# The transpose of a second norm vector goes to the side work of a hybrid decoder step, and its opening is reordered

## The chip, the core and the metric

The kernel runs on one core of a Trainium2 chip. Such a core has five engines, each with a queue of its own that it works off in order: TensorE (PE in the profile, with its weight loads as PEld), VectorE (DVE), ScalarE (ACT), GpSimd (POOL) and SyncE (SP). DMA transfers run beside them and are issued here by SP and ACT. The metric is the device time of one execution in microseconds (us); lower is better.

## The reference

One layer of a decoder trunk, for 1024 prompt positions and 8 x 8 sample positions, with a model width of 1024. Cut to what is computed:

```python
h = rmsnorm(x, g_norm)
bg_a, cg_a, v_a, z_a, a_b, g_b, z_b, q_x, z_x = split(h @ w_in)     # 1024 -> 3200 columns
out_a = bg_a * dwconv3(cg_a * v_a) * silu(z_a)
out_b = silu(layernorm(dwconv31(a_b * sigmoid(g_b)), ln_g, ln_b)) * silu(z_b)
m = rmsnorm(mem, g_mem)                                             # 256 memory tokens
out_x = softmax(q_x @ (m @ w_mk).T / 8) @ (m @ w_mv) * silu(z_x)    # 4 heads of 64
y = rmsnorm(x + concat(out_a, out_b, out_x) @ w_out, g_final)
```

The sample positions use cached keys, values and convolution states; the last states and the memory's keys and values are outputs too. Two norm vectors matter below: `g_norm`, which scales `x` ahead of the large projection, and `g_mem`, which scales the memory tokens.

## The kernel before

Everything lies transposed: 128 channels on the partitions, positions along a row. Each large product is made of three passes over a high and a low part of both operands (`hh`, `hl` for the activations, `wh`, `wl` for the weights): high times high, high times low weights, low activations times high weights. A part is split off by a rounding copy on ACT (or POOL) and a subtraction on DVE.

The 3200 columns of `w_in` are 25 blocks of 128 (`order`). For each block `n`, `proj` runs the three passes over eight row blocks `k` and the block is evacuated from PSUM by `evac`. The 1088 positions come in three chunks; the first five blocks (`NHEAD`) use the chunks of `HEAD`, 256, 384 and 448 positions. While `proj` runs, `side()` pops one entry of the list `steps` after every fourth product (two per pass): rescaling, splits of coming weights, parameter transposes, later the memory tokens (`mem_T`, which reads `gT[:, 8:16]`, from block 5 on), attention and the layer norm. The 31 taps of the long convolution are queued on DVE in the same way.

`startup` is the opening. It runs under `manual_schedule`: every engine does its instructions in the order in which they are written. It computes the first two chunks of the first four blocks and of block 4, and fills the third chunk's operands. Its course:

1. Loads. `graw` is an 8 x 128 tile that holds `g_norm` first and `g_mem` later. The first four blocks' weights come as eight row blocks of 128 x 512 (`hw_load`, tiles `hrw`), the first two rows of `x` as halves (`x_half`). SP issues all of them but the first `graw`, which ACT issues.
2. Five products on the identity, then the transpose of `graw` (L1012) and its copy to `gT[:, 0:8]`, then the transposes of `x` (`x0_tr`, four of eight `k` first) into PSUM banks.
3. Rows 0 and 1 of `x` aren't normalised ahead of the product. Their transposes times `g_norm` are split (`hi`, `lo`) and multiplied, group by group (`p(k, j)`: row block `k`, pass `j`, four products), while the squares are summed. The factors are brought in afterwards: `fb` holds them along rows, two transposes of `fb` give `rrow`, and the evacuations multiply by it.
4. In the same PSUM tile as those two transposes (`rps`) stands the transpose of `graw` with `g_mem`, and ACT copies `rrow` and `gT[:, 8:16]` out of it.
5. Row block 7's weights are split (`hw_hi(7)`, `hw_lo(7)`) behind that, its products end the first chunk, and the rows 2 to 4 of `x` are squared (`n1.square`), their factors computed (`n1.chain`, `n1.factor`) and applied (`n1.scale`). Block 4's weights are split (`w_hi`, `w_lo`), the four accumulators evacuated, block 4's three passes run, and the second chunk begins.

The profile's lines: L60 is every DVE operation (a wrapper), L96 every product (`mm`), L103 every transpose by `tr`, L276 the split copy of the row blocks, L188 a square on ACT, L238 `hi`, L176 and L210 loads of `x`, L270 and L293 loads of `w_in`.

## Time and profile before

| | us |
|---|---|
| median of 3 runs | 481.94 (481.22 to 482.19) |
| the profiled execution | 482.8 |
| its span, first to last instruction | 481.0 |
| busy: PE, DVE, ACT, POOL | 464.2, 324.4, 225.8, 7.1 |
| HBM read and written | 34.81 and 5.42 MB |

The granted PE clock averages 0.989 of full speed over the span. By stretches of the span, from the table of the trace by windows:

| stretch (us) | what runs | PE busy | DVE busy |
|---|---|---|---|
| 0 to 18.4 | first chunk up to the transposes of `fb` | 15.49 | 9.49 |
| 18.4 to 24.2 | | 0.24 | 0.04 |
| 24.2 to 33.2 | end of the first chunk, block 4 | 8.98 | 6.12 |
| 33.2 to 100 | other chunks, blocks 5 and on | 66.69 | 42.74 |
| 100 to 214 | long convolution beside products | 112.77 | 112.94 |
| 214 to 350 | attention, gates | 135.39 | 94.68 |
| 350 to 481 | output projection | 124.58 | 58.37 |

A busy PE is not a PE at its peak, since its products are pipelined; the idle time of an engine costs only where another waits for it.

### The profile page before, as it was taken

Reading aid. Unit: us, or ns where it says so; the run is one execution under the profiler, and the core shown is the slowest. Engines: PE = TensorE matmul, PEld = TensorE weight load, DVE = VectorE, ACT = ScalarE, POOL = GpSimd, SP = SyncE. Lnnn points to the kernel's source line nnn. Section 1 sums busy time; section 2 is a strip of 40 time slices with the busy share of each in tenths; the row PEclk is TensorE's granted clock in tenths of the full one; section 3 lists DMA queues with packets and bytes.
Section 4 is the critical chain, followed back from the end, with each engine's and each line's share of the span. In section 5 each row is a group of like instructions: output and inputs, shape, how many; then the busy total and the mean of one; then the engine's idle time right before and its main releaser. Section 6 shows DMA issues by size and latency. Waiting matters only on the chain.

```text
span 481.0 us, 7290 instructions
## 1 busy us (share of the span) xinstructions
PE 464.2 (97%) x2827; PEld 432.8 (90%) x2827; DVE 324.4 (67%) x573; ACT 225.8 (47%) x586; POOL 7.1 (1%) x22
## 2 busy tenths in 40 slices
PE   7599999999999999999999999999999999999994
PEld 7499999999999999899999999999999988888884
DVE  3465931999999999998679588832653446333434
ACT  5467722540625519655584374656863424221111
POOL 3001000000000000000000000000000000000000
PEclk9979999999999999999999999999999999999998
DMA  8940051121008300101111340113311562411111
GB/s 286 355 141 2 10 166 44 55 89 33 2 22 242 112 21 0 45 5 43 44 44 46 110 128 27 44 54 94 131 45 40 160 216 95 146 45 44 44 58 75
DMA packets 36446, 40.42 MB, mean 84 GB/s; under 512 B 1743, under 2 KB 30325, under 8 KB 36405
## 3 DMA queue, kind: packets, MB, share of 16 engines
q1 hardware_dynamic: 36397, 39.96, 26.1%
q8 instruction: 22, 0.36, 0.3%
q14 instruction: 11, 0.09, 0.1%
q10 hardware_dynamic: 16, 0.00, 0.0%
HBM read 34.81 MB, written 5.42 MB: 84 GB/s over the span
## 4 chain that ended last, share of the span: by engine, by line
PE 65%; DVE 22%; ACT 5%; DMA 4%; issue 3%; SPq 0%; DVEq 0%; ACTq 0%
PE mm L96 56%; DVE accB L60 11%; PE sd L103 4%; PE sd L96 4%; DMA graw<-in_g_mem_dram 2%; DVE tA L60 2%; DVE wl L60 2%; DMA x<-in_x_prompt_dram 1%; DVE Q L60 1%; DVE red L60 1%; DVE mx L60 1%; DMA wr<-in_w_in_dram 1%; ACT sd L870 1%; ACT junk L188 1%; DVE wml L60 1%
## 5 line engine op out<-in xcount | busy, mean ns | idle before, releaser
L96 PE MATMUL mm<-hh,wh 128*128 128x384 f32 (+3 forms) x592 | 117.0, 334 | 3.1 <-ACT wh L276 1.5
L96 PE MATMUL mm<-hl,wh 128*128 128x384 f32 (+3 forms) x592 | 117.6, 333 | 0.0
L60 DVE SCALAR_TENSOR_TENSOR accB<-u,prm,accB 128x1024 f32<-128x1024 f32 x90 | 115.0, 1279 | 1.2
L96 PE MATMUL mm<-hh,wl 128*128 128x384 f32 (+3 forms) x592 | 114.9, 331 | 0.0
L96 PEld LDWEIGHTS mm<-hh,wh 128*128 128x128 f32 x592 | 98.8, 189 | 6.6 <-ACT wh L276 1.8
L96 PEld LDWEIGHTS mm<-hl,wh 128*128 128x128 f32 x592 | 99.4, 190 | 2.0 <-issue 1.3
L96 PEld LDWEIGHTS mm<-hh,wl 128*128 128x128 f32 x592 | 99.9, 190 | 1.3 <-issue 0.3
L96 PE MATMUL mm<-woh,ml 128*128 128x512 f32 (+1 forms) x136 | 51.2, 377 | 0.0
L96 PE MATMUL mm<-wol,mh 128*128 128x512 f32 (+1 forms) x136 | 51.2, 377 | 0.0
L96 PE MATMUL mm<-woh,mh 128*128 128x512 f32 (+1 forms) x136 | 51.2, 377 | 0.0
L60 DVE TENSOR_TENSOR wl<-wr,wh 128x512 fp32r<-128x512 f32 x50 | 33.3, 685 | 10.0 <-ACT wh L276 7.4
L60 DVE TENSOR_TENSOR xres<-mm,xres 128x512 f32<-128x512 f32 (+2 forms) x19 | 12.4, 662 | 38.7 <-PE mm L96 38.5
L933 ACT ACTIVATE sd<-xres 128x512 f32<-128x512 f32 (+1 forms) x16 | 9.6, 600 | 56.9 <-DVE xres L60 56.9
L96 PEld LDWEIGHTS mm<-woh,mh 128*128 128x128 f32 x136 | 25.6, 188 | 4.7
L96 PEld LDWEIGHTS mm<-wol,mh 128*128 128x128 f32 x136 | 25.6, 188 | 4.7
L96 PEld LDWEIGHTS mm<-woh,ml 128*128 128x128 f32 x136 | 25.6, 188 | 4.6
L351 ACT ACTIVATE prod<-us,prm 128x64 f32<-128x64 f32 x93 | 23.9, 340 | 0.9 <-DVE wl L60 0.8
L701 ACT ACTIVATE P<-sd,nb 128x256 f32<-128x256 f32 x32 | 14.7, 473 | 18.8 <-DVE nb L60 18.8
L299 ACT CAST wh<-wr 128x512 fp32r<-128x512 f32 x40 | 23.3, 625 | 0.1
L499 ACT ACTIVATE sz<-mm 128x384 f32<-128x384 f32 (+1 forms) x24 | 11.3, 472 | 20.3 <-PE mm L96 20.2
L238 ACT ACTIVATE hh<-sd,gT 128x256 fp32r<-128x256 f32 (+2 forms) x24 | 12.8, 563 | 12.5 <-PE sd L103 12.2
L422 ACT ACTIVATE sig<-mm 128x384 f32<-128x384 f32 (+1 forms) x6 | 2.8, 472 | 31.3 <-PE mm L96 31.3
(204 smaller groups left out, 526.7 us busy)
## 6 DMA issues: line engine op xcount, KB each, us to landing
wr<-in_w_in_dram SPq DMA_DIRECT2D x21, 512.0 KB
wor<-in_w_out_dram SPq DMA_DIRECT2D x8, 512.0 KB
xres<-in_x_prompt_dram SPq DMA_DIRECT2D x8, 512.0 KB
out_dram<-xres SPq DMA_DIRECT2D x7, 512.0 KB
x<-in_x_prompt_dram SPq DMA_DIRECT2D x6, 512.0 KB
wr<-in_w_in_dram SPq DMA_DIRECT2D x8, 256.0 KB
cache<-in_cache_mem_k_dram SPq DMA_DIRECT2D x8, 256.0 KB
cache<-in_cache_mem_v_dram SPq DMA_DIRECT2D x8, 256.0 KB
```

What stands on the lines that cost most here:

```text
L60: r = f(*a, **k)
L96: T.matmul(out, lhsT, rhs, start=start, stop=stop)
L103: T.transpose(out, in_, ident[:n, :n])
L188: S.activation(junk[:r], self.ts[i][:r], AF.Square, accum_out=self.ss[:r, i:i + 1])
L238: S.activation(hh[k][:, off:off + n], ps[:, :n], AF.Copy, scale=gT[:, k:k + 1])
L299: S.copy(dst_hi[:, a:b], src[:, a:b])
L351: S.activation(p3[:, k, :], src, AF.Copy, scale=w[:, k0 + k:k0 + k + 1])
L422: S.activation(sig[j][:, off:off + n], ps[:, :n], AF.Sigmoid)
L499: S.activation(sz[0][:, off:off + n], ps[:, :n], AF.Silu)
L701: S.activation(P_[i][:, h * 256:h * 256 + 256], bank[h // 2][:, (h % 2) * 256:(h % 2) * 256 + 256], AF.Exp, bias=nb[:, h:h + 1], scale=SCA ...
L870: S.activation(junk[:, :384], t, AF.Square, bias=lst["nmu"][:, i:i + 1], accum_out=lst["sq"][:, i:i + 1])
L933: S.activation(junk[:rows], xr[:rows, cs], AF.Square, accum_out=ss[:rows, f:f + 1])
```

## The change

Five edits, all in the opening but for the side work's one new entry.

- The load of `g_mem` into `graw` moves on SP from behind the loads of `x` to behind `load_params()`. Its transpose and the copy to `gT[:, 8:16]` leave `rps`; the new `gm_T` does both, with a PSUM tile of its own and the copy on DVE, as the last of the entries that block 0 puts into `steps`.
- `x_half` and `hw_load` take a queue. SP issues the first half of row 0, weight row blocks 0 and 2, then the second halves; ACT issues the first half of row 1, `graw` with `g_norm`, weight row block 1, and then its first activation, which loads a table.
- The transposes of `x` for `k` = 4 to 7 stand on PE ahead of the groups `p(1, 1)` and `p(1, 2)`.
- Row 3's square moves from ACT to DVE (`square_v`), block 4's high parts from ACT to POOL. On DVE the scalings now stand ahead of block 4's low parts.
- Block 4's passes run in the order high times high, low activations times high weights, high times low weights.

```diff
+        def square_v(self, i):
+            junk = B("junk", cols=D)
+            V.tensor_tensor_reduce(
+                junk, self.ts[i], self.ts[i], 1.0, 0.0, ALU.mult, ALU.add, self.ss[:, i:i + 1]
+            )
+            dv(1130)
...
-    def x_half(i, h):
+    def x_half(i, h, q):
...
+    def gm_T():
+        ps = SD()
+        T.transpose(ps[:, 0:8], graw, ident[:8, :8])
+        V.tensor_copy(gT[:, 8:16], ps[:, 0:8])
...
-    def hw_load(k):
+    def hw_load(k, q=nc.sync):
...
     def startup():
+        V.memset(epst, EPS)
+        make_identity(nc, ident)
+        x_half(0, 0, nc.sync)
+        x_half(1, 0, nc.scalar)
+        hw_load(0)
         nc.scalar.dma_start(graw, g_norm[0].rearrange("(k p) -> k p", p=128))
-        V.memset(epst, EPS)
+        hw_load(1, nc.scalar)
         S.activation(warm, epst, AF.Sqrt)
-        make_identity(nc, ident)
+        hw_load(2)
         for i in (0, 1):
-            x_half(i, 0)
-        for k in range(3):
-            hw_load(k)
-        for i in (0, 1):
-            x_half(i, 1)
+            x_half(i, 1, nc.sync)
...
-        nc.sync.dma_start(graw, g_mem[0].rearrange("(k p) -> k p", p=128))
...
         p(2, 0)
-        p(1, 1)
-        p(1, 2)
         x_load(8)
         mem_load()
         load_params()
+        nc.sync.dma_start(graw, g_mem[0].rearrange("(k p) -> k p", p=128))
         w_load(5)
...
             for k in range(4, 8):
                 x0_tr(k, i)
+        p(1, 1)
+        p(1, 2)
...
                     tr(rps[:, i * 128:i * 128 + 128], fb[:, i * 128:i * 128 + 128], 128)
-                T.transpose(rps[:, 256:264], graw, ident[:8, :8])
                 n1.square(0)
                 rrow[0] = B("rrow", cols=RAW)
                 S.copy(rrow[0], rps[:, :RAW])
-                S.copy(gT[:, 8:16], rps[:, 256:264])
...
-        n1.square(1)
+        w_hi(4, G.tensor_copy)
+        n1.square_v(1)
         n1.square(2)
         n1.chain()
         n1.factor()
-        w_hi(4, S.copy)
+        n1.scale_act(1)
+        n1.scale(0)
+        n1.scale(2)
         w_lo(4)
-        n1.scale(0)
-        n1.scale_act(1)
-        n1.scale(2)
...
-        for j in range(3):
-            pass_(4, 0, pr4, j)
+        for j, (lo_, h) in enumerate(((False, hh), (False, hl), (True, hh))):
+            for k in range(KT):
+                mm(
+                    pr4[:, :RAW], w_block(4, k, lo_), h[k][:, :RAW],
+                    j == 0 and k == 0, j == 2 and k == KT - 1, RAW / 2.4,
+                )
...
                         steps += [mk(params_T, j), None]
+                    steps.append(gm_T)
```

## The prediction

> **What bounds the kernel now.** I began with the page: TensorE (PE) is busy nearly everywhere, and the chain that ended last (the last line) runs mostly through it, so time is to be won where PE stands still or runs slowly. The chain holds one oddity, a 4 KB load of `g_mem` with 2% of the span. (The middle line is DVE's busy tenths in 40 slices of 12 us.)

> ```profile
> PE 464.2 (97%) x2827; PEld 432.8 (90%) x2827; DVE 324.4 (67%) x573; ACT 225.8 (47%) x586; POOL 7.1 (1%) x22
> ...
> DVE  3465931999999999998679588832653446333434
> ...
> PE mm L96 56%; DVE accB L60 11%; PE sd L103 4%; PE sd L96 4%; DMA graw<-in_g_mem_dram 2%; DVE tA L60 2%; DVE wl L60 2%; DMA x<-in_x_prompt_dram 1%; DVE Q L60 1%; DVE red L60 1%; DVE mx L60 1%; DMA wr<-in_w_in_dram 1%; ACT sd L870 1%; ACT junk L188 1%; DVE wml L60 1%
> ```

> Next the same chain in order of time (start, duration, what). The first row is a weight load; then an `x` load lets the `g_mem` load go, which takes 9.20 us; the opening's products come behind it.

> ```profile
> 2.11 4.90 DMA wr<-in_w_in_dram
> 7.02 6.56 DMA x<-in_x_prompt_dram
> 13.67 9.20 DMA graw<-in_g_mem_dram
> ...
> 24.18 4.64 PE mm L96 x20
> 28.82 3.38 PE sd L96 x24
> ...
> 33.19 0.97 PE mm L96 x4
> ```

> Then the timeline around that load (start, duration, engine; in brackets idle time and what ended it).

> ```profile
> 16.53 0.64 PE L96 MATMUL mm<-hh,wh 128*128 128x256 f32 x4
> ...
> 17.01 0.64 PE L96 MATMUL mm<-hh,wl 128*128 128x256 f32 x4
> ...
> 17.97 0.38 PE L103 MATMUL sd<-ident,fb 128*128 128x128 f32 x2
> ...
> 22.91 0.23 PE L1094 MATMUL sd<-ident,graw 8*128 8x8 f32 x1 [4.56 <-DMA graw<-in_g_mem_dram]
> 23.17 0.37 ACT L1097 COPY rrow<-sd 128x256 f32<-128x256 f32 x1 [6.20 <-PE sd L1094]
> 23.44 0.17 ACT L1098 COPY gT<-sd 128x8 f32<-128x8 f32 x1
> 23.50 0.63 ACT L276 CAST wh<-wr 128x512 fp32r<-128x512 f32 x1
> 24.02 1.07 ACT L188 ACTIVATE junk<-x 128x1024 f32<-128x1024 f32 x1
> 24.16 0.69 DVE L60 TENSOR_TENSOR wl<-wr,wh 128x512 fp32r<-128x512 f32 x1 [6.64 <-ACT wh L276]
> 24.18 0.93 PEld L96 LDWEIGHTS mm<-hh,wh 128*128 128x128 f32 x4 [1.14 <-ACT wh L276]
> 24.18 1.22 PE L96 MATMUL mm<-hh,wh 128*128 128x256 f32 x4 [1.05 <-ACT wh L276]
> ...
> 26.24 0.17 DVE L60 TENSOR_SCALAR v<-ss 128x3 f32<-128x3 f32 x1 [1.39 <-ACT junk L188]
> ...
> 27.49 1.29 DVE L60 TENSOR_TENSOR wl<-wr,wh 128x512 fp32r<-128x512 f32 x2
> ...
> 28.70 1.53 DVE L60 TENSOR_SCALAR x<-x,y,t 128x1024 f32<-128x1024 f32 x2
> ...
> 30.14 1.08 DVE L60 TENSOR_TENSOR u<-mm,rrow 128x256 f32<-128x256 f32 x3
> ```

> PE is in order, so the transpose of `graw` for `g_mem`, which nothing needs before the memory tokens are transposed, stops PE; `rrow`'s copy reads the same PSUM tile and waits with it, and the split of the seventh weight row block stands behind that copy on ScalarE (ACT). From the transposes' end at 18.35 to 24.18 nothing useful runs. The table of stretches (duration, busy time by engine, then granted PE clock, DMA share, GB/s) shows the second cost.

> ```profile
> 22.50:23.00 0.50, 0.09 (x1) 0.09 (x1) 0.00 (x0) 0.00 (x0) 0.00 (x0) 1.00 0.79 238
> ...
> 24.00:25.00 1.00, 0.82 (x4) 0.82 (x5) 0.69 (x1) 1.00 (x3) 0.09 (x1) 0.50 0.91 168
> ...
> 29.50:29.75 0.25, 0.25 (x3) 0.25 (x3) 0.25 (x2) 0.00 (x0) 0.00 (x0) 0.50 0.62 154
> ...
> 30.00:30.50 0.50, 0.50 (x7) 0.50 (x6) 0.50 (x3) 0.00 (x0) 0.00 (x0) 1.00 0.95 344
> ```

> After the 4.56 us of idleness PE has half its clock until about 29.8: the 20 products from 24.18 to 28.41 take 0.21 us each, where four took 0.48 (16.53 to 17.01), 0.12 each, before it.

> **The change part by part.** *The opening.* First loads go out in pairs from SP and ACT.

> ```profile
> 0.73 0.58 ACTq L985 DMA_DIRECT2D graw<-in_g_norm_dram  x1
> ...
> 3.82 0.27 PE L1012 MATMUL mm<-ident,graw 8*128 8x8 f32 x1
> ...
> 4.02 1.97 PE L103 MATMUL sd<-ident,x 128*128 128x128 f32 x8
> ...
> 6.39 0.61 POOL L276 CAST wh<-wr 128x512 fp32r<-128x512 f32 x1 [5.01 <-DMA wr<-in_w_in_dram]
> ...
> 7.05 1.40 PE L96 MATMUL mm<-hh,wh 128*128 128x256 f32 x8 [1.06 <-POOL wh L276]
> ...
> 11.43 1.57 ACT L238 ACTIVATE hh<-sd,gT 128x256 fp32r<-128x256 f32 x4 [0.98 <-PE sd L103]
> ...
> 13.56 0.74 PE L96 MATMUL mm<-hh,wh 128*128 128x256 f32 x4 [0.41 <-ACT wh L276]
> ```

> The stretch of the first loads, in the columns of the table above:

> ```profile
> 4.00:7.00 3.00, 1.99 (x9) 1.47 (x8) 1.04 (x3) 0.84 (x2) 0.61 (x1) 1.00 1.04 333
> ```

> The first product waits for weight block 0, landed some 0.04 before 6.39. Issuing it one place sooner saves one issue, at most the 0.58 of ACT's row, but the DMA engines are full (share 1.04), and blocks 0 and 1, now on two queues, may finish together: block 1 landed at 7.01 (2.11 + 4.90), so 0.66 later is the bad end, 0.58 earlier the good one. `g_norm`'s load goes behind one `x` half on ACT, 0.5 to 1 us later; its transpose stands ahead of all of PE's, but the first product has 1.06 us of slack behind them. I take 0.3 late for all of it. The eight transposes placed ahead of two groups of products let ACT start its four evictions about 1 us sooner (0.98 of idleness there), which removes the 0.41 that PE waits at 13.56. Net 0.1 early, bounds 0.8 early and 1.0 late. ACT's table load, pushed back by its three issues, ends by 3.7, before ACT's first work at 5.39.

> [...] No run here shows two busy queues yet.

> *The transpose moved.* I call R the start of PE's products for the last row block: 24.18 now. Without `graw`, `rrow` is copied when the two `fb` transposes end, 18.35 (17.97 + 0.38), and from the start of that copy to PE's restart it is 24.18 - 23.17 = 1.01 us, less some 0.06 for the `gT` copy that leaves ACT (23.50 - 23.44). So R = 18.38 + 0.95 = 19.33, 4.85 earlier. What would be late next is a load, so I look at SyncE (SP): its loads wait for older ones. First its list of waits (total, times, longest), then its timeline:

> ```profile
> SPq L595 <- DMA wr<-in_w_in_dram: 1.4, 1, 1.4
> ```

> ```profile
> 18.01 0.34 SPq L595 DMA_DIRECT2D mem<-in_mem_prompt_dram  x1
> ```

> The second memory load went out at 18.01, when a `wr` load landed after 1.4 us of waiting. I read that as `w_load(4)`, the last `wr` before it; the last row block's load left SP two loads sooner, so it is in by then and ACT can cast it at 18.6. `x` rows 3 and 4 left SP before `w_load(4)` too.

> *The stretch behind the restart.* PE alone at full clock would need 20 products (2.4 us), 24 more for column block 4 (2.9), the last one's tail (four take 0.64, 0.16 past their slots) and the 1.0 of transposes and eviction from there to the next products (28.82 + 3.38 = 32.2 to 33.19): R + 6.4. VectorE (DVE) becomes the bound instead. Its new order is: low part of the last row block 0.69, square 1.4, the small chain 1.25 (26.24 to 27.49), two scalings 1.44 (28.70 to the next operation at 30.14), then the low part of block 4, first half 0.6 later, second 1.2 (27.49 to 28.70). It ends at R + 6.0, the first half at R + 5.4. The square on DVE has no row before; it reads two 1024-wide operands, like the tap.

> ```profile
> L60 DVE SCALAR_TENSOR_TENSOR accB<-u,prm,accB 128x1024 f32<-128x1024 f32 x90 | 115.0, 1279 | 1.2
> L60 DVE TENSOR_REDUCE red<-prod 128x64 f32<-128x1024 f32 x3 | 6.0, 1987 | 0.0
> ```

> I take 1.28 and a little for its sum; bounds 0.8 (a scaling, two in 1.53) and 2.0 (the reduction). ACT's square of row 4 runs beside it (1.07 at 24.02 for its like) and hides. The high part of block 4 on GpSimd is two casts of 0.61, from 18.0 to 19.2, hidden before R + 2.4, when PE asks for it; without GpSimd the two would stand on ACT ahead of the square. Block 4's first two passes now need no low part, so PE does 16 products to R + 4.3, waits for R + 5.4, does four (0.48), then four more from R + 6.0 to 6.64 with their tail, and 1.0 later starts the next column chunk at R + 7.7. DVE's evacuations (three in 1.08, so 1.44 for four) end at R + 7.4, under that cover. Today it is 33.19 = R + 9.0. So this stretch gives another 1.3, half of what PE alone would gain.

> *What is added later.* `gm_T` is one transpose on PE in side work, 0.14 to 0.23 us, and a DVE copy of 0.17 (the `gT` row's length) near 65 us, where DVE is idle two thirds of the time (the 3 and 1 in its sixth and seventh slice). Its load now goes out on SP after nine parameter loads, ahead of `w_load(5)`, which leaves 0.34 later, one issue; that block is cast only in the side work behind the opening, so this hides. If the cover were gone it would cost those 0.34. I count 0.15.

> *The sum:* 4.85 + 1.3 + 0.1 - 0.15 = **6.1 us**. From 33 us on I see no load that is late (the parameters' loads, due by then, are used in side work still later), so every later stage moves by the whole. The profiled execution took 482.8 with a span of 481.0; it becomes 476.7 and 474.9. The median of the runs shown is 0.9 lower, 481.94, so I forecast **475.8**.

> **The rivals.** *PE stays at half clock* (chance 0.10): two waits remain, about 1.0 us before R and 1.1 inside block 4. If they too halve the clock, the stretch behind R keeps its 9.0, the 1.3 falls away: 477.1. Against it: 1.06 us of idleness ended at 7.05, and the stretch of 4 to 7 us has a clock of 1.00. [...]

> *The opening loses a microsecond* (0.12): both first weight blocks late and `g_norm` later than its slack; R is then 20.3, 3.85 + 1.3 - 0.15 = 5.0, and the time 476.9.

> *DVE is quicker* (0.11): the square costs 0.8, so that the next chunk starts at R + 7.2, and the opening gains its 0.8; then 4.85 + 1.8 + 0.8 - 0.15 = 7.3, and 474.6.

> *Slower* (0.04): `g_norm`'s 4 KB behind a busy queue take what `g_mem`'s took, 9.20 from issue. PE's transposes then start at 10.5, the first product at about 12.3, 5.2 late, and PE, idle from 3.9, runs its next 5.6 us at half clock, 2.8 more. R is 27.2, 3.0 later than today, and 3.0 - 1.3 + 0.15 makes it 1.9 slower: 483.8. It decides if that load lands after some 8.5 us. Against it: one load of 256 KB is ahead of it on ACT, two of 256 and five of 512 KB were unlanded ahead of the other.

> *The change does not do what it says* (0.03): another wait holds `rrow` or the cast until 24, so nothing moves: 481.9.

> **How the numbers follow.** The forecast has 0.60, from 475.0 to 476.7. The range, 473.8 to 478.5, takes in the half clock, the late opening, the square's upper bound and most of the better case; outside lie the last two rivals and a little of the tails. A difference of 0.2%, 1 us, is about what a measurement here can tell from none. Faster 0.93, same 0.03, slower 0.04.

> **What would show it.** Right: no 4.56 us wait of PE near 18; the wait before R about 1 us; no 0.50 in the clock's column; R near 19.2 and the next chunk's first products near 26.9; DVE, not PE, busy without a gap from 19 to 25; PE's 0.41 wait for `wh` gone. Wrong: first products later than 7.7, a `graw` wait of PE near 4 to 6 longer than the slack, or clock 0.50 behind any short wait.

## The result, and the profile after

| | before | after |
|---|---|---|
| median (runs side by side, four of each), us | 481.58 (480.65 to 482.19) | 477.31 (477.14 to 477.76) |
| the profiled execution, us | 482.8 | 477.41 |
| its span, us | 481.0 | 475.3 |
| mean granted PE clock | 0.989 | 0.997 |

The ratio of the times is 0.9901, with a 95% interval from 0.9883 to 0.9919: faster by 1%, 4.3 us between these medians and 4.5 against 481.84, the median of 17 further runs of the kernel before, timed beside the first experiments. The forecast, 475.8, was 1.5 too low; the gain was to be 6.1. From profile to profile the span fell by 5.7.

The page of the changed kernel: busy times, granted PE clock in slices of 12 us, and the chain that ended last by line.

```profile
PE 462.9 (97%) x2827; PEld 431.1 (91%) x2827; DVE 325.5 (68%) x576; ACT 223.6 (47%) x581; POOL 8.2 (2%) x24
...
PEclk9999999999999999999999999999999999999998
...
PE mm L96 58%; DVE accB L60 11%; PE sd L103 5%; PE sd L96 3%; DVE wl L60 2%; DVE tA L60 2%; DVE Q L60 1%; DVE red L60 1%; DVE mx L60 1%; ACT sd L882 1%; DVE x L60 1%; ACT junk L188 1%; DMA wr<-in_w_in_dram 1%; DVE wml L60 1%; DMA graw<-in_g_norm_dram 1%
```

PE still sets the time and is busy for nearly as long as before, 462.9 us. What went is the chain's `g_mem` load with its 2%; the load of `g_norm` is a new link of it. The timeline of the changed kernel shows its opening, the stretch around the restart, and the moved transpose (start, duration, engine, what; idle time before it and what ended it).

```profile
4.73 0.27 PE L1025 MATMUL mm<-ident,graw 8*128 8x8 f32 x1 [0.84 <-DMA graw<-in_g_norm_dram]
...
5.94 0.61 POOL L288 CAST wh<-wr 128x512 fp32r<-128x512 f32 x1 [4.56 <-DMA wr<-in_w_in_dram]
...
17.75 1.17 POOL L319 CAST wh<-wr 128x512 fp32r<-128x512 f32 x2 [8.28 <-DMA wr<-in_w_in_dram]
...
17.96 0.38 PE L103 MATMUL sd<-ident,fb 128*128 128x128 f32 x2
18.38 0.37 ACT L1109 COPY rrow<-sd 128x256 f32<-128x256 f32 x1 [1.73 <-PE sd L103]
18.65 0.62 ACT L288 CAST wh<-wr 128x512 fp32r<-128x512 f32 x1
...
19.30 0.69 DVE L60 TENSOR_TENSOR wl<-wr,wh 128x512 fp32r<-128x512 f32 x1 [2.10 <-ACT wh L288]
...
19.32 0.74 PE L96 MATMUL mm<-hh,wh 128*128 128x256 f32 x4 [0.98 <-ACT wh L288]
...
19.91 1.22 DVE L60 CUSTOM_DVE_ANT_0 junk<-x 128x1024 f32<-128x1024 f32 x1
...
21.06 0.08 DVE L60 DVE_READ_ACCUMULATOR2_ANT ss<- 128x1 f32 x1
...
23.90 1.29 DVE L60 TENSOR_TENSOR wl<-wr,wh 128x512 fp32r<-128x512 f32 x2
...
24.64 1.35 PE L96 MATMUL sd<-hh,wl 128*128 128x256 f32 x8 [0.75 <-DVE wl L60]
...
26.98 0.97 PE L96 MATMUL mm<-hh,wh 128*128 128x384 f32 x4
...
67.87 0.97 PE L96 MATMUL mm<-hl,wh 128*128 128x448 f32 x4
...
68.77 0.22 PE L230 MATMUL sd<-ident,graw 8*128 8x8 f32 x1
...
69.84 0.36 PE L96 MATMUL mm<-hh,wh 128*128 128x448 f32 x1
```

Read it down the `[...]`. The transposes of `fb` end at 18.34, as they did before (18.35). Now ACT copies `rrow` at once and PE restarts at R = 19.32 instead of 24.18, 4.86 earlier, after 0.98 us of waiting. DVE then works from 19.30 to the end of block 4's low part at 25.19 almost without a gap; PE waits 0.75 for it, and the next chunk starts at 26.98, R + 7.66, where it started at 33.19, R + 9.0. So the 6.21 gained by then are 4.86 and 1.35. Two stretches of the changed kernel (duration, busy time by engine, granted clock, DMA share, GB/s) show what is left of the hole, and what follows it:

```profile
18.40:19.30 0.90, 0.00 (x0) 0.00 (x0) 0.00 (x0) 0.90 (x3) 0.59 (x2) 1.00 0.98 396
...
27.00:100.00 73.00, 72.89 (x421) 68.96 (x422) 48.65 (x105) 38.14 (x86) 2.40 (x2) 1.00 0.24 71
```

From the next chunk to 100 us PE stands still for 0.11 us in all, the same as before (66.8 of stretch, 66.69 busy): nothing new waits there. What the move costs stands at 68.77. In the timeline of the kernel before, the same eight products run unbroken:

```profile
74.03 1.78 PE L96 MATMUL mm<-hl,wh 128*128 128x448 f32 x8
75.65 1.58 PE L96 MATMUL mm<-hh,wh 128*128 128x448 f32 x7
```

There 1.62 us lie between the eight products' start and the next group; in the changed kernel, with the transpose among them, it is 69.84 - 67.87 = 1.97, so the transpose costs 0.35 though PE works on it for 0.22.

### The profile page after: what moved, and what is told of

The parts are those of the page before. It is cut to its first block, busy times and chain, and to the rows that moved or that the text cites. A ratio compares the mean times of both kernels' runs of the same rounds, so it can differ in the third digit from the quotient of the medians.

```text
span 475.3 us, 7295 instructions
## 1 busy us (share of the span) xinstructions
PE 462.9 (97%) x2827; PEld 431.1 (91%) x2827; DVE 325.5 (68%) x576; ACT 223.6 (47%) x581; POOL 8.2 (2%) x24
## 4 chain that ended last, share of the span: by engine, by line
PE 67%; DVE 23%; ACT 5%; issue 3%; DMA 2%; ACTq 0%; DVEq 0%; SPq 0%
PE mm L96 58%; DVE accB L60 11%; PE sd L103 5%; PE sd L96 3%; DVE wl L60 2%; DVE tA L60 2%; DVE Q L60 1%; DVE red L60 1%; DVE mx L60 1%; ACT sd L882 1%; DVE x L60 1%; ACT junk L188 1%; DMA wr<-in_w_in_dram 1%; DVE wml L60 1%; DMA graw<-in_g_norm_dram 1%
## 5 line engine op out<-in xcount | busy, mean ns | idle before, releaser
L96 PE MATMUL mm<-hh,wh 128*128 128x384 f32 (+3 forms) x592 | 117.1, 334 | 1.6 <-ACT wh L288 1.0
L96 PE MATMUL mm<-hl,wh 128*128 128x384 f32 (+3 forms) x592 | 116.8, 332 | 0.0
L60 DVE SCALAR_TENSOR_TENSOR accB<-u,prm,accB 128x1024 f32<-128x1024 f32 x90 | 115.2, 1281 | 1.2
L96 PE MATMUL mm<-hh,wl 128*128 128x384 f32 (+3 forms) x592 | 113.9, 330 | 0.0
L96 PEld LDWEIGHTS mm<-hh,wh 128*128 128x128 f32 x592 | 99.1, 190 | 5.2 <-ACT wh L288 1.5
L96 PEld LDWEIGHTS mm<-hl,wh 128*128 128x128 f32 x592 | 98.3, 188 | 2.0 <-issue 1.3
L96 PEld LDWEIGHTS mm<-hh,wl 128*128 128x128 f32 x592 | 99.0, 188 | 1.3 <-issue 0.3
L96 PE MATMUL mm<-woh,ml 128*128 128x512 f32 (+1 forms) x136 | 51.2, 377 | 0.0
L96 PE MATMUL mm<-wol,mh 128*128 128x512 f32 (+1 forms) x136 | 51.2, 377 | 0.0
L96 PE MATMUL mm<-woh,mh 128*128 128x512 f32 (+1 forms) x136 | 51.2, 377 | 0.0
L60 DVE TENSOR_TENSOR xres<-mm,xres 128x512 f32<-128x512 f32 (+2 forms) x19 | 12.4, 662 | 39.4 <-PE mm L96 39.2
L60 DVE TENSOR_TENSOR wl<-wr,wh 128x512 fp32r<-128x512 f32 x50 | 33.3, 686 | 5.1 <-ACT wh L288 2.7
L96 PEld LDWEIGHTS mm<-woh,mh 128*128 128x128 f32 x136 | 25.6, 188 | 4.7
L96 PEld LDWEIGHTS mm<-wol,mh 128*128 128x128 f32 x136 | 25.6, 188 | 4.7
L96 PEld LDWEIGHTS mm<-woh,ml 128*128 128x128 f32 x136 | 25.6, 188 | 4.6
```

The costliest lines, as they stand in the source:

```text
L60: r = f(*a, **k)
L96: T.matmul(out, lhsT, rhs, start=start, stop=stop)
```

## Experiments: the kernel before once more, and its parts

Three questions were open: why a span 5.7 shorter is worth only 4.3 to 4.5 in the medians; what each edit is worth; what limits the kernel now. The experiments ran in three groups, on different chips; the kernel before, timed beside each, had medians of 481.84, 481.86 and 482.01 us, so medians of different groups are compared below.

**The kernel before, unchanged**, profiled again and timed in 12 more runs.

> The kernel before, unchanged. Between the two profiled executions the span falls by 5.7 us, between the medians the time falls by 4.3. Theory A: the half-clock stretch after the 4.56 us wait is not equally long in every execution of the kernel before; the profiled one (clock 0.50 from 23.0 to 29.9) was an expensive one. Then spans lie between about 479.3 and 481.0, the longer ones with a lower mean granted clock (0.989 at 481.0, nearer 0.995 at 479.5). Rival B: the clock is the same 0.989 in all, and the profiled execution was longer for another reason; then spans differ without the clock.

Measured: 482.05 (480.87 to 483.45), ratio 1.0001 [0.9991, 1.0012]; this profiled execution has a span of 479.7, 1.3 less than the first. Its chain in order of time, and stretches of its clock:

```profile
13.69 8.86 DMA graw<-in_g_mem_dram
...
23.86 3.60 PE mm L96 x20
27.46 3.41 PE sd L96 x24
```

```profile
25.20:28.50 3.30, 3.30 (x17) 3.30 (x17) 2.28 (x9) 3.17 (x6) 0.00 (x0) 0.50 0.35 131
28.60:32.00 3.40, 3.38 (x29) 3.15 (x29) 3.11 (x8) 0.76 (x2) 0.00 (x0) 1.00 0.78 228
```

Beside them, the first profile of the same kernel:

```profile
19.62:23.02 3.40, 0.11 (x1) 0.11 (x1) 0.00 (x0) 0.00 (x0) 0.00 (x0) 1.00 1.03 337
23.04:26.44 3.40, 2.35 (x11) 2.26 (x12) 0.86 (x2) 3.24 (x8) 0.25 (x2) 0.50 0.97 254
26.45:29.85 3.40, 3.40 (x18) 3.40 (x17) 3.14 (x9) 2.27 (x4) 0.00 (x0) 0.50 0.25 78
```

Behind the wait PE ran at half clock for two stretches of 3.4 us in the first execution (the full clock is back in the prediction's row for 30.00), in this one for one. The wait itself was 4.56 us there and 2.72 here, as the transposes of `fb` ended later, at 19.87. R is 23.86 here, the products of the next chunk begin at 23.86 + 3.60 + 3.41 + 0.98 and a little, 31.87, which is R + 8.0 and not R + 9.0. Against this execution the changed kernel gains 23.86 - 19.32 = 4.54 up to R and 8.01 - 7.66 = 0.35 behind it, and loses 0.35 at the transpose: some 4.5, and its span is 479.7 - 475.3 = 4.4 shorter. That is what the medians show. The 29 spans of the kernel before that were taken with this run go from 478.7 to 481.7 with a median of 480.1: the execution on which the prediction's sum was made lay 0.9 above it. The mean clock sorts these spans only loosely: those at 0.988 and 0.989 lie between 479.7 and 480.9, those at 0.995 between 478.7 and 480.3, and the longest two, 481.3 and 481.7, have 0.992. The two profiled executions have 0.989 both. The opening's clock (full from 5.96 and from 11.51) and the landing of `g_mem` (22.87 and 22.55) vary too.

**The moved transpose alone**, on the kernel before:

```diff
-        nc.sync.dma_start(graw, g_mem[0].rearrange("(k p) -> k p", p=128))
...
         load_params()
+        nc.sync.dma_start(graw, g_mem[0].rearrange("(k p) -> k p", p=128))
...
-                T.transpose(rps[:, 256:264], graw, ident[:8, :8])
...
-                S.copy(gT[:, 8:16], rps[:, 256:264])
...
+                    steps.append(gm_T)
```

> The kernel before with the transpose of g_mem moved alone (its load behind the parameters' loads, gm_T in the side work). Theory A: it brings nearly all. R, PE's first products for the last row block, at 19.3; from there the old order of the squares, scalings and splits ends about as soon as the new one: next chunk at R + 7.2 to 7.5, 26.7; span 474.8, time 476.9 to 477.3. Rival C, the reordering of the stretch behind R is needed for the gain: next chunk at R + 8.5 or later, span 476 or more.

Measured: 477.53 (476.21 to 478.37), ratio 0.9904 [0.9885, 0.9923]. That is the whole gain, within what can be told. Its timeline:

```profile
19.52 0.38 PE L103 MATMUL sd<-ident,fb 128*128 128x128 f32 x2
...
20.88 0.74 PE L96 MATMUL mm<-hh,wh 128*128 128x256 f32 x4 [0.98 <-ACT wh L281]
...
28.23 0.97 PE L96 MATMUL mm<-hh,wh 128*128 128x384 f32 x4
```

The next chunk begins at R + 7.35 with the old order of the stretch, as expected. But R is 20.88 and not 19.3, and the span 476.5: the transposes of `fb` end at 19.90 in this execution, 1.55 later than in the first profile of the kernel before, and PE has its full clock only from 11.16 us on, where in that profile it has it from 5.96 on. This profiled run was the slowest of the four. The end of the experiments comes back to the clock in the opening.

**The changed kernel with the old order behind the restart** (squares of rows 2 and 3 and block 4's high parts on ACT, low parts ahead of the scalings, old order of the passes):

```diff
-        w_hi(4, G.tensor_copy)
-        n1.square_v(1)
+        n1.square(1)
         n1.square(2)
         n1.chain()
         n1.factor()
+        w_hi(4, S.copy)
+        w_lo(4)
+        n1.scale(0)
         n1.scale_act(1)
-        n1.scale(0)
         n1.scale(2)
-        w_lo(4)
...
+        for j in range(3):
+            pass_(4, 0, pr4, j)
```

> The changed kernel with the stretch behind R in its old order (squares on ACT, high parts of block 4 on ACT, low parts ahead of the scalings, old order of passes). Theory A: the same as the changed kernel within 0.4 us, next chunk at R + 7.2 to 7.5 against R + 7.66 measured. Rival C: 1 us or more slower than the changed kernel.

Measured: 477.61 (476.55 to 478.64), 0.9915 [0.9898, 0.9932]. The timeline of its profile:

```profile
19.21 0.74 PE L96 MATMUL mm<-hh,wh 128*128 128x256 f32 x4 [0.98 <-ACT wh L288]
...
26.55 0.96 PE L96 MATMUL mm<-hh,wh 128*128 128x384 f32 x4
```

The next chunk starts at R + 7.34, as in the run before it: at full clock the old order reaches the next chunk 0.3 sooner than the new one (R + 7.66), not later. The medians, 477.61 and 477.31, can't tell the two apart. The 1.35 that the changed kernel won behind R came from the clock.

**The changed kernel with the old opening**: old loads, and the eight transposes back behind the two groups.

```diff
...
+        for i in (0, 1):
+            x_half(i, 0, nc.sync)
+        for k in range(3):
+            hw_load(k)
...
         p(2, 0)
+        p(1, 1)
+        p(1, 2)
...
                 x0_tr(k, i)
-        p(1, 1)
-        p(1, 2)
```

> The changed kernel with the old loads and the old place of the eight transposes in the opening. Theory A: the new opening lost 0.9 us to the later g_norm load and 0.6 to the slow first products and got them back at the removed 0.41 wait and the earlier transposes, so it is worth nothing: R again at 19.3, span within 0.3 of 475.3, first products at 7.05. Rival D: the new opening is worth its 0.4 or more; then R at 19.7 or later.

Measured: 478.28 (477.57 to 479.06), 0.9929 [0.9915, 0.9943], about 1.0 slower than the changed kernel, though the two intervals just overlap. In its profile R is 19.94, which is what rival D gave, but PE has its full clock only from 9.96 on, in the changed kernel from 8.64, so that R alone doesn't measure the edit. PE's wait is back in its timeline:

```profile
14.17 0.74 PE L96 MATMUL mm<-hh,wh 128*128 128x256 f32 x4 [0.41 <-ACT wh L288]
```

**The changed kernel with the old loads alone**, the early transposes kept:

```diff
-        x_half(1, 0, nc.scalar)
...
-        hw_load(1, nc.scalar)
...
+        for i in (0, 1):
+            x_half(i, 0, nc.sync)
+        for k in range(3):
+            hw_load(k)
```

> The changed kernel with the old order and queues of the first loads, but the eight transposes still early. Theory A: PE's transposes end at 6.0, wait about 0.9 for weight block 0, and the gap keeps the clock low in some executions; where the clock rises at the same time as in the changed kernel, R is within 0.3 of 19.3; median 0.3 to 1.0 slower than the changed kernel. Rival D: the loads are worth nothing, the early transposes are the opening's whole gain: the same median within 0.3.

Measured: 477.58 (477.0 to 478.4), 0.9919 [0.9892, 0.9945]. The new queues are worth nothing that can be told. The early transposes may be worth up to 0.7 (478.28 to 477.58), but these two intervals overlap; what the traces show is that the wait of 0.41 is gone with them. In its profile R is 18.87, yet the next chunk starts at 26.94, as in the changed kernel (26.98). The reason stands in its timeline:

```profile
18.32 1.70 POOL L319 CAST wh<-wr 128x512 fp32r<-128x512 f32 x2 [8.21 <-DMA wr<-in_w_in_dram]
...
18.87 0.74 PE L96 MATMUL mm<-hh,wh 128*128 128x256 f32 x4 [0.98 <-ACT wh L288]
...
19.46 1.63 DVE L60 CUSTOM_DVE_ANT_0 junk<-x 128x1024 f32<-128x1024 f32 x1
```

GpSimd's two casts start when `w_load(4)` lands, which does not move with R: at 18.32 here, with R at 18.87, and at 17.75 in the changed kernel, with R at 19.32. Here they run while DVE squares: both take longer (1.70 for 1.17, 1.63 for 1.22), and DVE, which sets the next chunk, is where it was.

Medians of the four combinations, with `old opening` as the old loads and the old place of the transposes:

| | old order behind R | new order |
|---|---|---|
| old opening | 477.53 | 478.28 |
| new opening | 477.61 | 477.31 |

Four runs of one kernel spread over 0.6 to 2.2 us. So the transpose is worth 4.3, and the four reorderings together 0.2 more, with no sign that is sure.

**`g_norm` first on ACT**, since PE waits 0.84 for it at 4.73:

```diff
         x_half(0, 0, nc.sync)
+        nc.scalar.dma_start(graw, g_norm[0].rearrange("(k p) -> k p", p=128))
         x_half(1, 0, nc.scalar)
         hw_load(0)
-        nc.scalar.dma_start(graw, g_norm[0].rearrange("(k p) -> k p", p=128))
```

> The changed kernel with the load of g_norm issued first on ACT, ahead of the x half. Theory A: PE's transposes of x start at 4.0 instead of 4.94, the first products at about 6.6 instead of 6.93 (then bounded by weight block 0), R 0.3 earlier, span about 475.0 in an execution whose clock rises at the same time. Rival F: the loss behind a later start is covered anyway, R stays at 19.3. Whichever holds, spans will differ by about 1 us between executions, since the clock's rise in the opening now counts.

Measured: 478.96 (478.64 to 479.68), 0.9948 [0.9935, 0.9961]: 1.6 slower than the changed kernel, a miss. Its timeline:

```profile
3.82 0.27 PE L1025 MATMUL mm<-ident,graw 8*128 8x8 f32 x1
...
5.06 0.61 POOL L288 CAST wh<-wr 128x512 fp32r<-128x512 f32 x1 [3.68 <-DMA wr<-in_w_in_dram]
...
6.59 1.12 PE L103 MATMUL sd<-ident,x 128*128 128x128 f32 x4 [1.46 <-DMA x<-in_x_prompt_dram]
...
7.73 1.19 PE L96 MATMUL mm<-hh,wh 128*128 128x256 f32 x4
```

The vector came 0.9 earlier and weight block 0 too, but the half of `x` behind it on ACT came late: PE waited 1.46 for that, and the first products start at 7.73 instead of 6.93. The trace's first change to full clock stands at 12.6, in the changed kernel at 8.6, and R is 21.77. How much of the 1.6 is the late load and how much the late clock is not shown. Issuing one load sooner made another late.

## Experiments: the clock in the wait, and a better kernel

**The kernel before with the wait filled.** 18 products of the identity, into a PSUM tile that nobody reads, stand ahead of the transpose of `graw`: the wait stays, the half clock behind it should go.

```diff
+BUSY = 18
...
+                spare = SD()
+                for _ in range(BUSY):
+                    T.matmul(spare[:, :128], ident, ident, start=True, stop=True)
                 T.transpose(rps[:, 256:264], graw, ident[:8, :8])
```

> The kernel before, its wait for g_mem kept, with 18 products on the identity written into a spare PSUM tile behind the transposes of fb, so that PE is busy while it waits. This separates the slow clock from the wait. Theory A: no 0.50 behind the wait; PE's restart stays near 24.0, the next chunk follows at R + 7.3 (31.3) instead of 33.19 and 31.9 in the two profiles of the kernel before; spans about 479.2 and less spread than 478.7 to 481.7. Rival G: DVE bounds that stretch so far that the clock is worth nothing there; spans stay at 480.0 in the median.

Measured: 481.93 (480.31 to 483.21), 1.0 [0.9988, 1.0012]; no stretch of 0.50 behind R. Its timeline:

```profile
19.50 4.18 PE L1097 MATMUL sd<-ident 128*128 128x128 f32 x36
...
24.89 0.74 PE L97 MATMUL mm<-hh,wh 128*128 128x256 f32 x4 [1.05 <-ACT wh L277]
...
32.25 0.97 PE L97 MATMUL mm<-hh,wh 128*128 128x384 f32 x4
```

At full clock the old order needs R + 7.36 again, so the half clock alone cost 1.6 in the first execution (R + 9.0) and 0.65 in the second (R + 8.0). But in this execution PE came to the wait later (the transposes of `fb` end at 19.67, against 18.35), and the added products ran until 23.6, so that R is 24.89, 0.7 later than 24.18 and 1.0 later than 23.86. What the one gave, the other took: the spans, 478.5 to 481.4 with a median of 480.0, are those that rival G gave and not the expected 479.2, though not for its reason, since at full clock this stretch is shorter. The median leaves open what the half clock costs in a typical execution.

**More products ahead of the opening** (`WARM` is the number of products on the identity at the start), on the changed kernel:

```diff
-WARM = 5
+WARM = 7
```

> The changed kernel with 7 instead of 5 products on the identity and nothing else. Theory A: the clock's rise comes earlier, the opening shortens by 0.3 to 1.0, span 474.2 to 475.0. Rival I: 475.3 as before.

Measured: 477.17 (476.94 to 478.17), 0.9907 [0.9889, 0.9925]: no difference. In its profile PE has its full clock from 4.68 on instead of 8.64, R is 19.02, 0.30 earlier, and the next chunk 0.03 earlier, at 26.95. As with the old loads, DVE met GpSimd's casts (18.25 to 19.42) and its first low part took 0.97 instead of 0.69.

**What limits the stretch, moved out of the way.** If DVE's order and the late casts bound the stretch behind R, then work that needs neither belongs ahead of R. On the changed kernel: row block 7's high part and the squares of rows 2 to 4 go on ACT ahead of the copy of `rrow`, block 4's low part ahead of the small chain, and `g_mem` gets a tile of its own, loaded early by ACT and transposed beside `fb`, so that `gm_T` falls away. `WARM` is 7.

```diff
+    graw2 = cst.tile([8, 128], F32, name="graw2")
...
         hw_load(1, nc.scalar)
+        nc.scalar.dma_start(graw2, g_mem[0].rearrange("(k p) -> k p", p=128))
...
+                T.transpose(rps[:, 256:264], graw2, ident[:8, :8])
                 n1.square(0)
+                hw_hi(7, S.copy)
+                n1.square(1)
+                n1.square(2)
                 rrow[0] = B("rrow", cols=RAW)
...
         w_hi(4, G.tensor_copy)
-        n1.square_v(1)
-        n1.square(2)
+        w_lo(4)
         n1.chain()
...
-                    steps.append(gm_T)
```

> The loads of the changed kernel, the moved work of the version meant to beat both (own tile for g_mem, last cast and squares ahead of rrow's copy, low parts of block 4 ahead of the chain), and 7 instead of 5 products on the identity ahead of g_norm's transpose, so that PE has no gap from 1.4 us on. Theory A: the clock rises with the first of the equal stretches of 3.41 us in which PE never idles, so between 4.8 and 8.2 instead of 8.1 to 11.6; the next chunk starts 6.5 behind R, R is the end of fb's transposes; spans 472.0 to 473.2, time 474 to 475.2. Rival I, what fills the gap delays PE by as much as the clock gives: spans as in the run with 5.

Measured: 475.28 (474.62 to 475.64), 0.9864 [0.9841, 0.9886].

**The same with `WARM` at 5:**

> The same with 5 products, so with the gap of 0.8 us before g_norm's transpose. Theory A: 0.3 to 1 us slower in the median than with 7. Rival I: the same median.

Measured: 474.87 (474.72 to 476.51), 0.9867 [0.9845, 0.9888]. The two can't be told apart, so the products at the start are worth nothing here: in the two profiles PE has its full clock from 4.40 and from 8.96 on, yet the next chunk starts at 25.30 and 25.09. Both are about 7 us faster than the kernel before and 2.0 to 2.4 faster than the changed one. The timeline of the second:

```profile
18.41 0.22 PE L1109 MATMUL sd<-ident,graw 8*128 8x8 f32 x1
...
18.56 0.74 PE L96 MATMUL mm<-hh,wh 128*128 128x256 f32 x4
...
18.91 1.17 POOL L320 CAST wh<-wr 128x512 fp32r<-128x512 f32 x2 [9.38 <-DMA wr<-in_w_in_dram]
...
19.56 1.67 DVE L60 TENSOR_TENSOR wl<-wr,wh 128x512 fp32r<-128x512 f32 x2 [1.49 <-POOL wh L320]
...
25.09 0.97 PE L96 MATMUL mm<-hh,wh 128*128 128x384 f32 x4
```

PE goes from the transposes to the products without a wait, and the next chunk starts at R + 6.53, near the R + 6.4 that the prediction gave for PE alone. The waits of 0.98 and 0.75 are gone, which with the 0.35 of the moved transpose makes 2.1.

**A variant of it with `g_norm` first on ACT**, as in the slower kernel above, and three more products on the identity behind the first eight transposes to fill its gap:

```diff
         x_half(0, 0, nc.sync)
+        nc.scalar.dma_start(graw, g_norm[0].rearrange("(k p) -> k p", p=128))
         x_half(1, 0, nc.scalar)
...
                 x0_tr(k, i)
+        for _ in range(3):
+            T.matmul(wps[:, :128], ident, ident, start=True, stop=True)
```

> A version meant to beat both: g_norm first on ACT; g_mem in a tile of its own, loaded by ACT behind weight block 1 and transposed beside fb, so that gm_T goes; the last row block's cast and the squares of rows 3 and 4 ahead of rrow's copy on ACT; block 4's high parts on GpSimd and its low parts ahead of the chain on DVE; three products on the identity behind the first eight transposes to keep PE busy up to the first product. Theory A: R at about 18.1, right behind the transposes of fb, no DVE wait in block 4, next chunk at 24.6 to 25.5 against 26.98; span 472.3 to 473.3, time 474.2 to 475.3. Rival H, another load is late or ACT becomes the bound: next chunk at 26 or later, span over 474.3.

Measured: 475.08 (474.69 to 476.01), 0.9863 [0.9848, 0.9877]: the same as the two above. In its profile R is 19.80 and the next chunk starts at 26.34, later than the expected 24.6 to 25.5; PE has its full clock only from 10.84 on there, and this run was the slowest of the four.

**The same without the three products:**

> The same without the three products on the identity. Theory A: the clock may fall back in the opening in some executions, as it did in one profile of the kernel before; so the fastest span is that of the version with them, within 0.3, and the median is later by up to 0.7. Rival: no difference in median or spread.

Measured: 476.83 (475.55 to 478.17), 0.9904 [0.9889, 0.9919], 1.75 slower. Stretches of its clock:

```profile
4.85:8.24 3.39, 1.57 (x10) 0.95 (x8) 0.92 (x3) 1.04 (x3) 3.15 (x6) 1.00 1.02 364
8.26:11.66 3.40, 2.95 (x14) 2.95 (x15) 2.70 (x6) 3.19 (x7) 0.11 (x1) 0.50 1.00 321
11.68:15.08 3.40, 3.40 (x31) 3.40 (x31) 2.30 (x6) 2.31 (x6) 0.00 (x0) 1.00 1.02 393
```

With a gap in it, PE is busy for 1.57 of 3.39 us, and in the next stretch its clock is 0.50. The price of it is seen in the spans of these runs, 473.7 at a mean clock of 0.998 and 476.1 and 476.3 at 0.989, and not in the two profiles, where the next chunk starts at 26.61 without and 26.34 with the three products. It was more than expected: the fastest span is 0.8 longer than that of the version with them, 472.9, and the median 1.75. That nothing later waits for a load that would hide it is the likely reason, not a tested one.

**Across all fourteen profiles** the end of the transposes of `fb` goes with the moment from which PE keeps its full clock in the opening. In the seven where that is 4.4 to 9.0 us, they end between 17.9 and 18.5, and how early the clock comes makes no clear difference; in the seven where it is 10.0 to 12.6, they end between 19.0 and 20.8. The unchanged kernel before is found on both sides, with 18.35 in its first profile (5.96) and 19.87 in its second (11.51), and so differs with the execution. The five profiles with the changed kernel's opening are all on the early side, four of the five with the old one on the late side. Whether the new opening brings the clock earlier or these executions happened to, is not shown, so what the edits of the opening are worth stays open too.

## Why the prediction was right, and where its size was off

- **The wait removed, 4.85: right.** It measured 4.86, by the terms given: the copy of `rrow` at 18.38, ACT's cast from 18.65, 0.94 from copy to restart. No other load stood behind the wait, and R was forecast at 19.33 and came at 19.32. That it hit so closely is in part luck: the terms from the transposes of `fb` on are sound, but their end was taken from one execution with an early full clock, and in the run with the moved transpose alone the same terms lead to 20.88.
- **The opening, 0.1 early: nothing came of it** by the transposes of `fb` (18.34 against 18.35), but this pair doesn't measure it, as the full clock begins at 5.96 before and at 8.64 after. `g_norm` came 0.91 later (its transpose at 4.73 against 3.82), the upper half of the 0.5 to 1 that was allowed for, and the first products' slack took it. PE's 0.41 is gone. Weight block 0 came near the good end of its bounds (0.58 earlier to 0.66 later): its cast starts at 5.94 against 6.39, 0.45 earlier.
- **The stretch behind the restart, R + 7.7: right; its worth of 1.3: only against that one execution.** DVE's order ended as forecast (square 1.22 and 0.08 against "1.28 and a little"; R + 5.9 against R + 6.0), the waits were 0.98 and 0.75 against 1.0 and 1.1, and the clock held. This is the step that failed: the 9.0 from which 7.7 was taken held two stretches at half clock, and the kernel profiled again has one and R + 8.0, so that 0.35 is left of the 1.3. The new order itself gave nothing: the old one at full clock needs 7.34 to 7.36.
- **`gm_T`, 0.15: it is 0.35.** The price of the instruction was counted, not that of the weight load for it, below.
- **From 33 us on the whole gain is kept: right.** 6.21 at the next chunk less 0.35 makes 5.86; the span fell by 5.7.
- **From the profiled execution to the median: wrong.** The whole 6.1 was taken from a median whose executions the sum had not been made against. Of the 1.6 by which 4.5 falls short of it, 0.4 was missing in the profiles already (6.1 to 5.7); 0.9 is the profiled span's distance from the 480.1 of its like (the changed kernel's 475.3 lies among its four, 475.0 to 475.7); and some 0.3 lies outside the span, 2.1 us in the changed kernel's profiled run and 1.8 in that of before. The cause of this last part stays open. Kernels that share the new loads have either value.

By its number alone, 477.31 lies outside the 475.0 to 476.7 of the forecast proper and nearest to the rival of the half clock, at 477.1. That is chance: of the rivals, the half clock behind shorter waits did not come in the changed kernel's profile, nor did the late opening, the quick square or the slow `g_norm` (its load took 3.52 from 1.17, not 9.20). One argument against the half clock was a misreading: the 1.00 for 4 to 7 us was no full clock up to 5.96, where the trace has its first clock record, for the eight transposes at 4.02 take 1.97 and eight like them at 10.69 take 1.03. That the first execution of before was an expensive one was no rival, and the 0.9 us between the two times shown was its sign. That a typical execution of before has the one slow stretch of the second profile is the likely reading of the medians, but it rests on two profiles; filling the wait did not settle it.

## What to carry to other kernels

When an instruction that nothing needs yet waits for a load on an in-order engine (4.56 us of PE here), move it out of that queue: here that one edit was the gain, 4.3, and what to look for next is the engine or the load that sets the work right behind it. Make the sum against a typical execution: if the profiled one lies above the median, find which of its stalls vary (here a half clock of one stretch or two) before taking a gain from the median. A wait for a load also hides what varies ahead of it, so the opening's losses count only once the wait is gone: with it R was 24.18 and 23.86 where the full clock began at 5.96 and 11.51, without it 19.32 and 20.88 where that was 8.64 and 11.16.

## What the runs showed of the hardware

```profile
4.69:8.10 3.41, 1.76 (x14) 1.37 (x13) 1.90 (x4) 1.88 (x5) 1.56 (x2) 1.00 1.01 330
8.10:11.51 3.41, 3.41 (x19) 3.41 (x18) 2.38 (x5) 2.38 (x5) 1.72 (x4) 0.50 1.04 404
```

```profile
4.69:8.09 3.40, 2.07 (x15) 1.55 (x14) 1.69 (x5) 1.54 (x4) 1.98 (x3) 1.00 1.08 389
8.10:11.50 3.40, 3.40 (x29) 3.40 (x30) 2.67 (x6) 3.40 (x8) 1.31 (x3) 1.00 0.97 381
```

The first pair also shows what the wait hid: a step at half clock in the opening, from 8.10, and yet R came at 23.86, set by the landing of `g_mem`, not later than in the other execution. These steps are the likely reason why the wait for `g_mem` cost two slow steps in one execution and one in another: the first slow step of the first profile still held a part of the wait (1.05 us of idleness up to R) and was followed by another, the one of the second profile held none and was the last.

**Where GpSimd's casts and DVE's two-operand work overlapped, the one that began second took longer** in the three profiles that follow. With the old loads, two casts took 1.70 for 1.17, the second of them beginning within a subtraction, and a square that began within that cast 1.63 for 1.22. In the better kernel with `WARM` at 5 a pair of subtractions took 1.67 for 1.29, and in the changed kernel with seven products one subtraction 0.97 for 0.69; both began within a cast, and the casts kept their 1.17.

**The small transpose among large products cost more than itself**, 0.35 for the 0.22 that PE works on it. In the changed kernel the weight loads for the products at 67.87 and 69.84 start 0.20 ahead of them, at 67.67 and 69.64, beside the products before; that of the 8 x 128 tile starts with its transpose, at 68.77. The timeline of the changed kernel's weight loads:

```profile
68.77 0.13 PEld L230 LDWEIGHTS sd<-ident,graw 8*128 8x128 f32 x1 [0.30 <-issue]
```

PEld stands idle for 0.30 ahead of it, with nothing that the profile shows to wait for, until about the end of the last product before it (67.87 + 0.97 = 68.84).
